# Layer 0's kept halves, a later flag branch and a shorter exact search in a two-layer attention and convolution kernel

## The chip, the cores and the metric

The kernel runs on one core of a Trainium2 chip. The metric is the time of one execution in microseconds (us) on the device. The engines are TensorE (PE, its weight loads PEld), VectorE (DVE), ScalarE (ACT), GpSimd (POOL) and SyncE (SP), which here issues the DMA transfers.

## The reference

2048 tokens of width 1024 pass two layers and a final norm. Layer 0 ("even") is sparse attention with 8 heads, in which an indexer selects the 256 best earlier positions for each token, beside a gated convolution of 31 taps; layer 1 ("odd") is a gated convolution of 3 taps. Cut to what matters here:

```python
def dsa_attention(q, k, v, q_idx, k_idx, w_idx):   # blocks of 128 queries
    dots = einsum('bqhd,bsd->bqhs', qib, kif)
    score = einsum('bqh,bqhs->bqs', wb, relu(dots))
    score = where(key_pos <= t, score, -inf)
    _, sel = lax.top_k(score, 256)
    ...                                  # softmax(q k) v over the selected positions

def odd_layer(h, w_in, conv_w, w_out):
    b_gate, c_gate, xin, gate = split(h @ w_in, 4)
    y = b_gate * causal_depthwise_conv(c_gate * xin, conv_w)
    return (y * silu(gate)) @ w_out

h = x
h = h + even_layer(rms_norm(h, g0), ...)
h = h + odd_layer(rms_norm(h, g1), ...)
return rms_norm(h, final_g)
```

## The kernel before, in words

Tokens are worked on in four chunks of 512 (16 blocks of 128). Weights and activations are fp32 values split into two fp16 halves, high and low, and each product of two of them takes three matmuls (`mm3`, L187 to L189, 24 matmuls for a projection onto 128 rows). Halves are named `xh`/`xl` (the normed input of layer 0), `mh`/`ml` (what goes into layer 0's output projection), `nh`/`nl` (the normed input of layer 1) and `yh`/`yl` (layer 1's product).

**Order.** The program is written as generators, each of which yields after a step. `weave(main, steps, (fill, rate), ...)` runs a main generator and, after each of its steps, so many steps of each fill as its rate says: `CN0` for the convolution of the next chunk, `R2` for the attention of chunk 1. `paced` ties an instruction to a matmul of the main generator, for the order alone. From this program a scheduler with a time model makes one list per engine, and an engine works off its list in order.

**Selection.** For most blocks the threshold of the 256 best is found by counting steps on ACT (L794) and a selection of candidates on DVE (L819 to L841), which ends by adding to `bad` whether a block was not settled. For blocks 2 and 3, and in a conditional fallback for all others, `general` (L276 to L317) finds it exactly: 31 bits of the threshold, one after the other; for each bit the scores of every block are compared with a trial threshold and counted (L292, once per block), the count is compared with 256 (L293), and the trial is kept or dropped (L304). Two more instructions per bit (L294, L295) keep the largest count below 256, and L302 turns the trial into a float's bits.

**From layer 0 to layer 1.** After layer 0's last attention, `fl`, `fps` and `fi` (L983 to L988) reduce `bad` to one flag. `last_gates` (L1117 to L1133) makes the last projections of layer 0 from chunk 3's halves, which it loads again from `xs_dr` into tiles of the pool `l1` (L1121, L1122). `out_even(0)` is the output projection of chunk 0, `norm_odd` the norm ahead of layer 1, whose `row_diag` ends in `rs_d` (L163) and whose `spread` multiplies that out (L169). Then the flag is loaded into a register on every engine (L1147) and a branch (L1148) skips the fallback, which isn't taken here; the keys and values of the attention are loaded (L1165, L1166). The loop over chunks follows: `odd` in 16 steps of two projections (48 matmuls) is woven with the attention of the next chunk (32 heads over four blocks; scores L1171, softmax L346 to L356 on DVE, ACT and POOL, transposing DMA L358, value products L379, transposed result L403). `out_even(1)` needs that attention's result as `mh`/`ml` (L182, L183).

Of the kernel before, what the change touches and what calls it, by code (L numbers as in the profile page):

```python
# [12 lines left out]
FP32 = mybir.dt.float32  # L13
# [8 lines left out]
P = 128  # L22
# [22 lines left out]
LOOK = 2  # L45
ATR = 3.5
CE, CX, CN0, CNR, R0, R1, R2 = 1.5, 3.0, 1.0, 0.85, 1.65, 1.65, 2.5
# [26 lines left out]
def trunk_kernel(ctx: ExitStack, tc: tile.TileContext, xT, pos, wE, woE, wO, woO, par, tab, outT):  # L74
# [38 lines left out]
    stg = ctx.enter_context(tc.tile_pool(name="stg", bufs=2))  # L113
    w_dr = {}
# [159 lines left out]
    def general(scs, get):  # L274
# [3 lines left out]
        def small(name, dt=FP32):  # L278
            return get(name, TT, dt)[:, 0:nb]

        cur, tr, bits, xm, acc = small("cur", I32), small("try", I32), small("bits", I32), small("xm", I32), small("acc", I32)
        cnt, cg, tmp, zero, izero = small("cnt"), small("cg"), small("tmp"), small("zero"), small("izero", I32)
        V.memset(cg, 0.0)
        V.memset(zero, 0.0)
        V.memset(izero, 0)
        V.memset(xm, 0x7FFFFFFF)
        V.memset(cur, -2 ** 31)

        def count(th):
            for n, b in enumerate(bl):  # L290
                junk = get("junk", wmax, BF16)
                V.tensor_scalar(out=junk[:, 0:(b + 1) * P], in0=scs[b], scalar1=th[:, n:n + 1], scalar2=0.0, op0=ALU.is_ge, op1=ALU.add, accum_out=cnt[:, n:n + 1])  # L292
            V.tensor_scalar(out=acc, in0=cnt, scalar1=float(TOPK), scalar2=None, op0=ALU.is_ge)  # L293
            V.scalar_tensor_tensor(out=tmp, in0=cnt, scalar=float(TOPK), in1=cnt, op0=ALU.is_lt, op1=ALU.mult)  # L294
            V.tensor_tensor(out=cg, in0=cg, in1=tmp, op=ALU.max)  # L295

        count(zero)
        V.copy_predicated(out=cur, mask=acc, data=izero)
        V.copy_predicated(out=xm, mask=acc, data=izero)
        for bit in range(30, -1, -1):  # L300
            V.tensor_scalar(out=tr, in0=cur, scalar1=1 << bit, scalar2=None, op0=ALU.bitwise_or)
            V.tensor_tensor(out=bits, in0=tr, in1=xm, op=ALU.bitwise_xor)  # L302
            count(bits.bitcast(FP32))
            V.copy_predicated(out=cur, mask=acc, data=tr)  # L304
        V.tensor_tensor(out=bits, in0=cur, in1=xm, op=ALU.bitwise_xor)
        thr = bits.bitcast(FP32)
# [121 lines left out]
    with ExitStack() as es:  # L428
        csp = es.enter_context(tc.tile_pool(name="csp", bufs=1))
        xp = es.enter_context(tc.tile_pool(name="xp", bufs=2))  # L430
# [549 lines left out]
        weave(rest(3, reload(3)), 99, (att, ATR))  # L980
        drain(att)

        fl = const.tile([P, 1], FP32, name="fl")  # L983
        V.tensor_reduce(out=fl, in_=bad, axis=mybir.AxisListType.X, op=ALU.max)
        fps = ps_m.tile([P, CH], FP32, name="ps_m")
        T.matmul(out=fps[:, 0:1], lhsT=ones, rhs=fl, start=True, stop=True)
        fi = const.tile([P, 1], I32, name="fi")
        V.tensor_scalar(out=fi, in0=fps[:, 0:1], scalar1=0.5, scalar2=None, op0=ALU.is_gt)  # L988
# [56 lines left out]

    def norm_all(x1, rb):
        nh = l1.tile([P, KD, CH], F16, name="nh", bufs=1)
        nl = l1.tile([P, KD, CH], F16, name="nl", bufs=1)
# [68 lines left out]
    def last_gates():  # L1117
        xh = l1.tile([P, KD, CH], F16, name="yh", bufs=1)
        xl = l1.tile([P, KD, CH], F16, name="yl", bufs=1)
        for k in range(0, KD, 4):  # L1120
            SP.dma_start(out=xh[:, k:k + 4, :], in_=xs_dr[NCH - 1][:, 0, k:k + 4])  # L1121
            SP.dma_start(out=xl[:, k:k + 4, :], in_=xs_dr[NCH - 1][:, 1, k:k + 4])  # L1122
# [21 lines left out]
    drain(late)  # L1144


    rv = nc.values_load(fi[0:1, 0:1], min_val=0, max_val=1)  # L1147
# [44 lines left out]
    for c in range(NCH):  # L1192
# [7 lines left out]
        yh = l1.tile([P, KD, CH], F16, name="yh", bufs=1)  # L1200
# [76 lines left out]
```

## Time and profile before

| | us |
|---|---|
| median of 3 runs | 2210.19 (2207.39 to 2213.84) |
| the profiled execution | 2207.73 |
| its span, first to last instruction | 2205.9 |
| PE busy in it | 1988.8 |
| DVE busy | 1657.8 |
| ACT busy | 1185.4 |
| POOL busy | 800.9 |

The profiled execution is one of its own; its time stands 1.8 us above its span and 2.5 us below the median of the runs. The mean granted clock of TensorE in it was 0.968 of full speed.

### The profile page before, as it was taken

The page shows a single profiled execution, that of the slowest core. Times are in us where ns is not written, and L with a number is a line of the kernel's source. Part 1 is how long each engine was busy: PE and PEld are TensorE (multiplying, and loading weights), DVE is VectorE, ACT ScalarE, POOL GpSimd, SP SyncE. Part 2 cuts the span into 40 slices and gives each one's busy share as a digit, 9 for nine tenths or more (in the row PEclk, how much of TensorE's full clock was granted, in tenths as well). Part 3 has the DMA queues.
Part 4 walks back from the last instruction along what each step waited for, and adds up shares of the span by engine and source line. Part 5 has one row for each costly group of instructions (what it writes and reads, how often), then busy time and mean ns, then how long its engine had stood idle before and what let it go on. Part 6 is the DMA issues. An engine that isn't in the chain of part 4 may idle for free. (4 is left out here: it accounts for less than half of the span.)

```text
span 2205.9 us, 34976 instructions
## 1 busy us (share of the span) xinstructions
PE 1988.8 (90%) x12252; PEld 1074.9 (49%) x12252; DVE 1657.8 (75%) x3580; ACT 1185.4 (54%) x2411; POOL 800.9 (36%) x761
## 2 busy tenths in 40 slices
PE   4877888898999898798998999999999999999997
PEld 3644464555454543344444444554554555444446
DVE  7999989999978694888874888874888887243224
ACT  5656665566577847467784654563554666121111
POOL 4765344435133321346662542441443455000000
PEclk9889999999999998999999999999999999999999
DMA  6445456333745376678896677776777788423234
GB/s 231 172 145 207 153 180 229 111 114 128 227 122 154 108 217 219 210 214 204 224 212 204 179 194 196 169 181 175 166 169 200 183 182 187 140 104 134 96 111 157
DMA packets 406052, 380.89 MB, mean 173 GB/s; under 512 B 313456, under 2 KB 333680, under 8 KB 385136
## 3 DMA queue, kind: packets, MB, share of 16 engines
q1 hardware_dynamic: 405872, 378.63, 60.5%
q8 instruction: 96, 1.57, 0.3%
q14 instruction: 84, 0.69, 0.1%
HBM read 216.45 MB, written 88.70 MB: 138 GB/s over the span
## 5 line engine op out<-in xcount | busy, mean ns | idle before, releaser
L356 POOL TENSOR_TENSOR pp<-lg,pp 128x512 f16<-128x512 f32 (+3 forms) x320 | 342.8, 1095 | 571.9 <-ACT pp L355 485.3
L187 PE MATMUL ps_w<-nh,wt 128*128 128x512 f16 x1024 | 391.1, 383 | 7.2 <-ACT wt L209 3.2
L188 PE MATMUL ps_w<-nl,wt 128*128 128x512 f16 x1024 | 392.0, 383 | 0.0
L189 PE MATMUL ps_w<-nh,wt 128*128 128x512 f16 x1024 | 389.2, 382 | 0.7 <-POOL wt L210 0.7
L187 PEld LDWEIGHTS <-wt 128*128 128x128 f16 x2112 | 208.3, 99 | 249.2 <-issue 23.4
L188 PEld LDWEIGHTS <-wt 128*128 128x128 f16 x2112 | 208.5, 99 | 242.1 <-issue 27.2
L189 PEld LDWEIGHTS <-wt 128*128 128x128 f16 x2112 | 208.6, 99 | 237.9 <-issue 11.2
L241 DVE SCALAR_TENSOR_TENSOR ps_c<-cin,cwt,ps_c 128x512 f32<-128x512 f32 x348 | 261.5, 752 | 30.8 <-ACT ps_c L239 26.9
L353 ACT ACTIVATE lg<-lg,m 128x512 f32<-128x512 f32 (+3 forms) x320 | 207.3, 649 | 120.4 <-DVE m L346 120.1
L210 POOL TENSOR_TENSOR wt<-w_stage,wt 128x512 f16<-128x512 f32 x136 | 167.9, 1241 | 262.3 <-ACT wt L209 248.5
L187 PE MATMUL ps_p<-xh,wt 128*128 128x512 f16 x480 | 185.1, 386 | 14.2 <-ACT th L222 5.9
L189 PE MATMUL ps_p<-xh,wt 128*128 128x512 f16 x480 | 184.0, 385 | 2.1 <-POOL wt L210 2.1
L188 PE MATMUL ps_p<-xl,wt 128*128 128x512 f16 x480 | 185.3, 386 | 0.0
L355 ACT CAST pp<-lg 128x512 f16<-128x512 f32 (+3 forms) x320 | 165.0, 550 | 21.9 <-DMA pt<-pp 17.2
L739 PE MATMUL ps_i<-ki,qst 128*128 128x512 f16 (+3 forms) x608 | 147.2, 363 | 32.7 <-ACT relu L741 32.1
L741 ACT ACTIVATE relu<-ps_i 128x1024 f32<-128x1024 f32 (+7 forms) x176 | 141.0, 811 | 65.0 <-DVE sc L743 39.3
L743 DVE SCALAR_TENSOR_TENSOR sc<-relu,wi,sc 128x1024 f32<-128x1024 f32 (+7 forms) x140 | 161.9, 1156 | 14.0 <-ACT relu L741 13.8
L187 PE MATMUL ps_p<-wt,xh 128*128 128x256 f16 (+1 forms) x608 | 167.9, 276 | 4.8 <-ACT u L598 2.5
L188 PE MATMUL ps_p<-wt,xh 128*128 128x256 f16 (+1 forms) x608 | 167.8, 276 | 0.6 <-POOL wt L210 0.6
L189 PE MATMUL ps_p<-wt,xl 128*128 128x256 f16 (+1 forms) x608 | 166.9, 276 | 0.1
L794 ACT ACTIVATE junk<-sc,t_x 128x640 bf16<-128x640 f32 (+5 forms) x84 | 118.8, 1414 | 65.2 <-DVE t_x L809 40.7
L1171 PE MATMUL ps_q<-kk,qs_a 128*128 128x512 f16 (+3 forms) x576 | 142.3, 356 | 4.4 <-DVE m L346 4.4
(293 smaller groups left out, 3851.2 us busy)
## 6 DMA issues: line engine op xcount, KB each, us to landing
wt<-w_in_wo_dram SPq DMA_DIRECT2D x48, 1024.0 KB, 5.1
wt<-w_in_we_dram SPq DMA_DIRECT2D x39, 1024.0 KB, 5.6
w_stage<-in_wo_dram SPq DMA_DIRECT2D x64, 256.0 KB, 3.5
w_in_wo_dram<-wt SPq DMA_DIRECT2D x16, 1024.0 KB, 4.9
wt<-w_in_woo_dram SPq DMA_DIRECT2D x16, 1024.0 KB, 5.0
w_in_we_dram<-wt SPq DMA_DIRECT2D x13, 1024.0 KB, 4.9
w_stage<-in_we_dram SPq DMA_DIRECT2D x48, 256.0 KB, 3.4
wt<-w_in_woe_dram SPq DMA_DIRECT2D x12, 1024.0 KB, 4.8
```

What stands on the lines that cost most here:

```text
L187: T.matmul(out=out, lhsT=sh(k), rhs=mh(k), start=k == 0, stop=False)
L188: T.matmul(out=out, lhsT=sh(k), rhs=ml(k), start=False, stop=False)
L189: state["mm"] = T.matmul(out=out, lhsT=sl(k), rhs=mh(k), start=False, stop=k == KD - 1)
L210: G.tensor_tensor(out=wt[:, 1, ks, :], in0=st, in1=wt[:, 0, ks, :], op=ALU.subtract)
L241: ins = V.scalar_tensor_tensor(out=out if t == CK - 1 else acc, in0=ci[:, t:t + CH], scalar=cwt[:, j, t:t + 1], in1=acc, op0=ALU.mult, op1 ...
L353: A.activation(out=e, in_=e, func=AF.Exp, bias=last, scale=-1.0, accum_out=blk["ss"][:, h, si:si + 1])
L355: A.copy(out=pp[:, 0:w], in_=e)
L356: eng.tensor_tensor(out=pp[:, w:2 * w], in0=e, in1=pp[:, 0:w], op=ALU.subtract)
L739: T.matmul(out=ps[:, r0:r0 + r], lhsT=qst[:, h, i * P:(i + 1) * P], rhs=ki[:, a, s0 + r0:s0 + r0 + r], start=a == 0, stop=a == 1)
L741: A.activation(out=rl[:, 0:w], in_=ps[:, 0:w], func=AF.Relu)
L743: V.scalar_tensor_tensor(out=sc[:, s0:s0 + w], in0=rl[:, 0:w], scalar=wi[:, b, h:h + 1], in1=tiny[:, s0:s0 + w] if h == 0 else sc[:, s0:s0 ...
L1171: ins = T.matmul(out=ps[:, 0:w], lhsT=qs[:, h, :], rhs=kk[:, a, s0:s0 + w], start=a == 0, stop=a == 1)
```

## The change

It does three things. (1) The pool `xp` of layer 0's halves lives on to the end of the kernel. The last pair that layer 0 loads (`held_last`) is handed to `last_gates`, which loads nothing any more, and the halves `nh`/`nl` and `yh`/`yl` of layer 1 are taken in turn from the same pool through `halves`. (2) The flag's reduction, its matmul and the branch stand after the first two steps of `odd` for chunk 0 (`ALONE`), so the loads of keys and values and the attention come behind that; those two steps are woven with the convolution only; the flag's matmul is tied to their last matmul. `R2` is 2.45 in place of 2.5. (3) `general` searches the float's own bits: it starts from -1, each trial flips one bit by exclusive or, and neither the mask `xm` nor the largest count below 256 is kept. The count above the threshold, which the last step needs, is taken once at the end, with `is_gt`.

```diff
@@ -43,8 +43,9 @@
 NCAND = 16
 NWT = 2
 LOOK = 2
+ALONE = 2
 ATR = 3.5
-CE, CX, CN0, CNR, R0, R1, R2 = 1.5, 3.0, 1.0, 0.85, 1.65, 1.65, 2.5
+CE, CX, CN0, CNR, R0, R1, R2 = 1.5, 3.0, 1.0, 0.85, 1.65, 1.65, 2.45
 ORDER = ('ggqgqg', 'ggqgqg', 'gggg', 'qq')
 EX = 1
 TQ, TP = 2, 4
@@ -111,6 +112,7 @@
     xs_dr = [dram.tile([P, 2, KD, CH], F16, name=f"xs_dr{c}") for c in range(NCH)]
     wp = ctx.enter_context(tc.tile_pool(name="wp", bufs=NWT))
     stg = ctx.enter_context(tc.tile_pool(name="stg", bufs=2))
+    xp = ctx.enter_context(tc.tile_pool(name="xp", bufs=2))
     w_dr = {}
     URGENT = {(wE.tensor.name, t) for t in (T_K, T_QI, T_KI)}
 
@@ -278,32 +280,29 @@
         def small(name, dt=FP32):
             return get(name, TT, dt)[:, 0:nb]
 
-        cur, tr, bits, xm, acc = small("cur", I32), small("try", I32), small("bits", I32), small("xm", I32), small("acc", I32)
-        cnt, cg, tmp, zero, izero = small("cnt"), small("cg"), small("tmp"), small("zero"), small("izero", I32)
-        V.memset(cg, 0.0)
+        cur, tr, acc = small("cur", I32), small("try", I32), small("acc", I32)
+        cnt, cg, zero, izero = small("cnt"), small("cg"), small("zero"), small("izero", I32)
         V.memset(zero, 0.0)
         V.memset(izero, 0)
-        V.memset(xm, 0x7FFFFFFF)
-        V.memset(cur, -2 ** 31)
-
-        def count(th):
+        V.memset(cur, -1)
+
+        def count(th, out, op):
             for n, b in enumerate(bl):
                 junk = get("junk", wmax, BF16)
-                V.tensor_scalar(out=junk[:, 0:(b + 1) * P], in0=scs[b], scalar1=th[:, n:n + 1], scalar2=0.0, op0=ALU.is_ge, op1=ALU.add, accum_out=cnt[:, n:n + 1])
+                V.tensor_scalar(out=junk[:, 0:(b + 1) * P], in0=scs[b], scalar1=th[:, n:n + 1], scalar2=0.0, op0=op, op1=ALU.add, accum_out=out[:, n:n + 1])
+
+        def keep(data):
             V.tensor_scalar(out=acc, in0=cnt, scalar1=float(TOPK), scalar2=None, op0=ALU.is_ge)
-            V.scalar_tensor_tensor(out=tmp, in0=cnt, scalar=float(TOPK), in1=cnt, op0=ALU.is_lt, op1=ALU.mult)
-            V.tensor_tensor(out=cg, in0=cg, in1=tmp, op=ALU.max)
-
-        count(zero)
-        V.copy_predicated(out=cur, mask=acc, data=izero)
-        V.copy_predicated(out=xm, mask=acc, data=izero)
+            V.copy_predicated(out=cur, mask=acc, data=data)
+
+        count(zero, cnt, ALU.is_ge)
+        keep(izero)
         for bit in range(30, -1, -1):
-            V.tensor_scalar(out=tr, in0=cur, scalar1=1 << bit, scalar2=None, op0=ALU.bitwise_or)
-            V.tensor_tensor(out=bits, in0=tr, in1=xm, op=ALU.bitwise_xor)
-            count(bits.bitcast(FP32))
-            V.copy_predicated(out=cur, mask=acc, data=tr)
-        V.tensor_tensor(out=bits, in0=cur, in1=xm, op=ALU.bitwise_xor)
-        thr = bits.bitcast(FP32)
+            V.tensor_scalar(out=tr, in0=cur, scalar1=1 << bit, scalar2=None, op0=ALU.bitwise_xor)
+            count(tr.bitcast(FP32), cnt, ALU.is_ge)
+            keep(tr)
+        thr = cur.bitcast(FP32)
+        count(thr, cg, ALU.is_gt)
         V.tensor_scalar(out=cg, in0=cg, scalar1=-1.0, scalar2=float(TOPK), op0=ALU.mult, op1=ALU.add)
         for n, b in enumerate(bl):
             W = (b + 1) * P
@@ -427,7 +426,6 @@
 
     with ExitStack() as es:
         csp = es.enter_context(tc.tile_pool(name="csp", bufs=1))
-        xp = es.enter_context(tc.tile_pool(name="xp", bufs=2))
         e1 = es.enter_context(tc.tile_pool(name="e1", bufs=2))
         p0 = es.enter_context(tc.tile_pool(name="p0", bufs=2))
         cvp = es.enter_context(tc.tile_pool(name="cvp", bufs=1))
@@ -977,15 +975,9 @@
         r2 = rest(2, reload(2))
         weave(r2, 99, (cn0, CE), (att, ATR))
         drain(cn0)
-        weave(rest(3, reload(3)), 99, (att, ATR))
+        held_last = reload(3)
+        weave(rest(3, held_last), 99, (att, ATR))
         drain(att)
-
-        fl = const.tile([P, 1], FP32, name="fl")
-        V.tensor_reduce(out=fl, in_=bad, axis=mybir.AxisListType.X, op=ALU.max)
-        fps = ps_m.tile([P, CH], FP32, name="ps_m")
-        T.matmul(out=fps[:, 0:1], lhsT=ones, rhs=fl, start=True, stop=True)
-        fi = const.tile([P, 1], I32, name="fi")
-        V.tensor_scalar(out=fi, in0=fps[:, 0:1], scalar1=0.5, scalar2=None, op0=ALU.is_gt)
 
 
     mx = ctx.enter_context(tc.tile_pool(name="mx", bufs=1, reuse_waits="tile"))
@@ -1043,9 +1035,11 @@
             state["gate"] = None
             return norm_all(x1, rb)
 
+    def halves():
+        return xp.tile([P, KD, CH], F16, name="xh"), xp.tile([P, KD, CH], F16, name="xl")
+
     def norm_all(x1, rb):
-        nh = l1.tile([P, KD, CH], F16, name="nh", bufs=1)
-        nl = l1.tile([P, KD, CH], F16, name="nl", bufs=1)
+        nh, nl = halves()
         for k in range(KD):
             xn = l1.tile([P, CH], FP32, name="xi")
             V.scalar_tensor_tensor(out=xn, in0=x1[:, k, :], scalar=g1[:, k:k + 1], in1=rb, op0=ALU.mult, op1=ALU.mult)
@@ -1115,11 +1109,7 @@
         return l1.tile([P, KD, CH], FP32, name="x1"), l1.tile([P, CH], FP32, name="ssum", bufs=1)
 
     def last_gates():
-        xh = l1.tile([P, KD, CH], F16, name="yh", bufs=1)
-        xl = l1.tile([P, KD, CH], F16, name="yl", bufs=1)
-        for k in range(0, KD, 4):
-            SP.dma_start(out=xh[:, k:k + 4, :], in_=xs_dr[NCH - 1][:, 0, k:k + 4])
-            SP.dma_start(out=xl[:, k:k + 4, :], in_=xs_dr[NCH - 1][:, 1, k:k + 4])
+        xh, xl = held_last
 
         def chan(wt, z):
             ps = ps_w.tile([P, CH], FP32, name="ps_w")
@@ -1142,8 +1132,19 @@
     drain(even)
     n = norm_odd(x1, acc, late)
     drain(late)
-
-
+    yh, yl = halves()
+    main = odd(*n, yh, yl)
+    weave(main, ALONE, (cnv, CN0))
+
+
+    fl = const.tile([P, 1], FP32, name="fl")
+    V.tensor_reduce(out=fl, in_=bad, axis=mybir.AxisListType.X, op=ALU.max)
+    fps = ps_n.tile([P, CH], FP32, name="ps_m")
+    state["gate"] = state["mm"]
+    paced(T.matmul(out=fps[:, 0:1], lhsT=ones, rhs=fl, start=True, stop=True))
+    state["gate"] = None
+    fi = const.tile([P, 1], I32, name="fi")
+    V.tensor_scalar(out=fi, in0=fps[:, 0:1], scalar1=0.5, scalar2=None, op0=ALU.is_gt)
     rv = nc.values_load(fi[0:1, 0:1], min_val=0, max_val=1)
     with tc.If(rv > 0):
         with tc.tile_pool(name="fb", bufs=1) as fb:
@@ -1197,9 +1198,9 @@
             weave(out_even(c, *m[c], x1, acc), 99, (cnv, CNR), (att, R0))
             n = norm_odd(x1, acc, late, (cnv, CNR), (att, R1))
             weave(late, 99, (cnv, CNR), (att, R1))
-        yh = l1.tile([P, KD, CH], F16, name="yh", bufs=1)
-        yl = l1.tile([P, KD, CH], F16, name="yl", bufs=1)
-        weave(odd(*n, yh, yl), 99, (cnv, CNR if c else CN0), (att, R1 if c else R2))
+            yh, yl = halves()
+            main = odd(*n, yh, yl)
+        weave(main, 99, (cnv, CNR if c else CN0), (att, R1 if c else R2))
         late = out_odd(c, x1, yh, yl, 2 if c + 1 == NCH else 1)
         drain(att)
         drain(cnv)
```

DVE near layer 1's first norm, before, in the program's order. `rs_a`, `rs_r` and `rs_t` are steps of the norm's reciprocal root, `fi` is the flag. The names behind the operation are output and inputs, then the output's shape.

```order
L148 SCALAR_TENSOR_TENSOR rs_t<-rs_t,rs_a 128x4
L149 SCALAR_TENSOR_TENSOR rs_r<-rs_t,rs_r 128x4
L147 TENSOR_TENSOR rs_t<-rs_r 128x4
L148 SCALAR_TENSOR_TENSOR rs_t<-rs_t,rs_a 128x4
L149 SCALAR_TENSOR_TENSOR rs_r<-rs_t,rs_r 128x4
L147 TENSOR_TENSOR rs_t<-rs_r 128x4
L988 TENSOR_SCALAR fi<-ps_m 128x1
L148 SCALAR_TENSOR_TENSOR rs_t<-rs_t,rs_a 128x4
L1147 TENSOR_LOAD fi
L1148 COMPARE_AND_BRANCH
```

And after the change, the same norm up to its end, where `fl` is the flag's reduction and `xi` the first normed rows of layer 1:

```order
L1141 TENSOR_REDUCE fl<-bad 128x1
L149 TENSOR_TENSOR rs_t<-rs_r 128x4
L150 SCALAR_TENSOR_TENSOR rs_t<-rs_t,rs_a 128x4
L151 SCALAR_TENSOR_TENSOR rs_r<-rs_t,rs_r 128x4
L149 TENSOR_TENSOR rs_t<-rs_r 128x4
L150 SCALAR_TENSOR_TENSOR rs_t<-rs_t,rs_a 128x4
L151 SCALAR_TENSOR_TENSOR rs_r<-rs_t,rs_r 128x4
L149 TENSOR_TENSOR rs_t<-rs_r 128x4
L150 SCALAR_TENSOR_TENSOR rs_t<-rs_t,rs_a 128x4
L151 SCALAR_TENSOR_TENSOR rs_r<-rs_t,rs_r 128x4
L165 SCALAR_TENSOR_TENSOR rs_d<-id_62,rs_r 128x512
L1045 SCALAR_TENSOR_TENSOR xi<-x_9786,par_sb,ps_m 128x512 x2
```

The flag's conversion, its load and the branch are gone from the middle of the norm; the line numbers after the change are one to two higher in the helpers (L163 is L165).

PE around the flag, before: the last products of `last_gates`, the flag's matmul, the branch, the norm's product and the first products of layer 1:

```order
L188 LDWEIGHTS wt
L188 MATMUL ps_w<-yl,wt 128x512
L189 LDWEIGHTS wt
L189 MATMUL ps_w<-yh,wt 128x512
L986 MATMUL ps_m<-fl,ones 128x1
L1147 TENSOR_LOAD fi
L1148 COMPARE_AND_BRANCH
L1148 UNCONDITIONAL_BRANCH x2
L169 MATMUL ps_m<-rs_d,ones 128x512
L187 LDWEIGHTS wt
L187 MATMUL ps_w<-nh,wt 128x512
```

And around the branch after the change, where the tiles of layer 1's first halves are now called `xh` and `xl`:

```order
L190 LDWEIGHTS wt
L190 MATMUL ps_w<-xl,wt 128x512
L191 LDWEIGHTS wt
L191 MATMUL ps_w<-xh,wt 128x512
L1148 TENSOR_LOAD fi
L1149 COMPARE_AND_BRANCH
L1149 UNCONDITIONAL_BRANCH x2
L189 LDWEIGHTS wt
L189 MATMUL ps_w<-xh,wt 128x512
L190 LDWEIGHTS wt
```

The branch stands among the products of layer 1's third step (117 of them are ahead of it, and 149 ahead of the first score product), the norm's product is far above it, and the flag's matmul 21 products above it.

PE near the end of `odd` for chunk 0, before: `a_nat` is the attention's last result, transposed here, and 68 products of `odd` still follow:

```order
L187 LDWEIGHTS wt
L187 MATMUL ps_w<-nh,wt 128x512
L188 LDWEIGHTS wt
L188 MATMUL ps_w<-nl,wt 128x512
L403 MATMUL ps_m<-id_62,a_nat 128x128 x4
L189 LDWEIGHTS wt
L189 MATMUL ps_w<-nh,wt 128x512
L187 LDWEIGHTS wt
L187 MATMUL ps_w<-nh,wt 128x512
L188 LDWEIGHTS wt
L188 MATMUL ps_w<-nl,wt 128x512
```

And after the change:

```order
L378 MATMUL ps_v<-vv,pt 128x128
L378 LDWEIGHTS pt
L378 MATMUL ps_v<-vv,pt 128x64
L378 LDWEIGHTS pt
L378 MATMUL ps_v<-vv,pt 128x128
L402 MATMUL ps_m<-id_62,a_nat 128x128 x4
L189 LDWEIGHTS wt
L189 MATMUL ps_w<-mh,wt 128x512
L189 LDWEIGHTS wt
L189 MATMUL ps_w<-mh,wt 128x512
```

The transposed result now stands at the very end, behind the last product of `odd`, the last score products and 48 value products (`ps_v`), and `out_even(1)` (`mh`, `ml`) follows it directly.

## Rows read from the trace of the kernel before

**Rows 1.** page, part 1: engine, busy us, share of the span, instructions.

```profile
PE 1988.8 (90%) x12252; PEld 1074.9 (49%) x12252; DVE 1657.8 (75%) x3580; ACT 1185.4 (54%) x2411; POOL 800.9 (36%) x761
```

**Rows 2.** windows: stretch, length; busy us of each engine (x count); clock, DMA share.

```profile
117.00:300.00 183.00, 144.14 (x808) 78.45 (x807) 180.25 (x554) 115.06 (x207) 85.66 (x81) 0.90 0.52 183
...
870.00:930.00 60.00, 56.25 (x263) 25.40 (x261) 55.98 (x96) 26.07 (x44) 19.78 (x16) 1.00 0.57 194
...
940.00:950.00 10.00, 8.51 (x27) 3.01 (x26) 8.80 (x14) 5.12 (x9) 0.17 (x1) 0.64 0.74 279
```

**Rows 3.** PE's waits, 117 to 300 us: sum in us, times, longest.

```profile
PE ps_t L633 <- DVE stk L620: 11.9, 3, 5.6
...
PE ps_i L739 <- ACT relu L741: 10.8, 10, 3.2
```

**Rows 4.** page, part 5: busy, mean ns | idle before it, main releaser.

```profile
L741 ACT ACTIVATE relu<-ps_i 128x1024 f32<-128x1024 f32 (+7 forms) x176 | 141.0, 811 | 65.0 <-DVE sc L743 39.3
```

**Rows 5.** PE's waits, 848 to 960 us.

```profile
PE ps_m L169 <- DVE rs_d L163: 10.2, 1, 10.2
...
PE ps_w L187 <- DMA yh<-xs_dr: 9.5, 1, 9.5
```

**Rows 6.** DVE's groups by form, 117 to 283 us: busy us, mean ns.

```profile
L295 DVE TENSOR_TENSOR s_cg<-s_cg,s_tmp 128x2 f32<-128x2 f32 x32 | 8.9, 278 | 0.0
...
L294 DVE SCALAR_TENSOR_TENSOR s_tmp<-s_cnt 128x2 f32<-128x2 f32 x32 | 8.0, 249 | 0.0
...
L302 DVE TENSOR_TENSOR s_bits<-s_try,s_xm 128x2 int32<-128x2 int32 x31 | 7.8, 250 | 0.5
```

**Rows 7.** DVE's timeline in the search: start, us, instruction.

```profile
260.16 0.17 DVE L293 TENSOR_SCALAR s_acc<-s_cnt 128x2 int32<-128x2 f32 x1
...
260.76 0.16 DVE L302 TENSOR_TENSOR s_bits<-s_try,s_xm 128x2 int32<-128x2 int32 x1
...
260.96 0.61 DVE L292 TENSOR_SCALAR_CACHE_REDUCE mk<-cv,s_bits 128x384 bf16<-128x384 f32 x1
```

**Rows 8.** timelines, ACT, then DVE, near the norm; in brackets the idle time before.

```profile
863.35 0.63 ACT L208 ACTIVATE w_stage<-w_stage 128x512 f32<-128x512 f32 x1 [3.04 <-DMA w_stage<-in_woe_dram]
...
864.54 1.89 ACT L794 ACTIVATE junk<-sc,t_x 128x1920 bf16<-128x1920 f32 x1
...
934.65 0.63 ACT L208 ACTIVATE w_stage<-w_stage 128x512 f32<-128x512 f32 x1 [6.39 <-SPq L1148]
...
936.83 0.35 DVE L149 SCALAR_TENSOR_TENSOR rs_r<-rs_t,rs_r 128x4 f32<-128x4 f32 x1 [5.14 <-DVEq L1148]
...
937.21 1.67 DVE L163 SCALAR_TENSOR_TENSOR rs_d<-id,rs_r 128x512 f32<-128x512 f32 x1
```

**Rows 9.** timelines of PE, DVE and ACT, chunk 1's attention.

```profile
942.57 1.01 PE L187 MATMUL ps_w<-nh,wt 128*128 128x512 f16 x2 [1.49 <-ACT nh L182]
...
955.17 0.92 PE L1171 MATMUL ps_q<-kk,qs_a 128*128 128x512 f16 x5
...
1147.45 0.59 PE L1171 MATMUL ps_q<-kk,qs_a 128*128 128x512 f16 x2
...
1151.87 0.74 DVE L346 CUSTOM_DVE_ANT_0 lg<-ps_q,mb_a,m 128x512 f32<-128x512 f32 x1
...
1153.74 0.71 ACT L353 ACTIVATE lg<-lg,m 128x512 f32<-128x512 f32 x1
...
1157.52 0.60 ACT L355 CAST pp<-lg 128x512 f16<-128x512 f32 x1
...
1172.97 0.69 DVE L183 TENSOR_TENSOR ml<-a_nat,mh 128x512 f16<-128x512 f32 x1 [0.69 <-ACT mh L182]
...
1189.51 0.38 PE L187 MATMUL ps_w<-mh,wt 128*128 128x512 f16 x1
...
1199.65 0.38 PE L189 MATMUL ps_w<-mh,wt 128*128 128x512 f16 x1
```

**Rows 10.** line L1147, the flag's load: duration in ns, start us.

```profile
L1147 ACTq TENSOR_LOAD <-fi x1: 1422/1422/1422, 931.6 to 931.6; - x1
```

## The prediction

> **What bounds the kernel now.** I read the engine totals first, then windows by stage, then who PE waits for, then timelines around the two places that the diff edits. PE is busy 1988.8 of 2205.9 us, DVE 1657.8 [rows 1]: over the whole PE is the bound, so only PE's idle time can be won. Windows show two stages in which DVE is the bound instead: from 117 to 300 us DVE is busy 180.25 of 183 and PE 144.14; from 870 to 930 us DVE has 55.98 of 60 [rows 2]. The first holds the exact search that `general` runs for blocks 2 and 3; the second ends in layer 0's last selection and the norm ahead of the odd layer. PE's two long waits in the first stage sum to 22.7 us: one goes to DVE directly [rows 3], the one for relu at second hand, since ACT's relu mostly waits for DVE's L743 [rows 4]. Around the second place PE has two waits, 9.5 us for the reloaded halves and 10.2 us for the norm's `rs_d` [rows 5].
>
> **Search, 31 bits.** L294, L295 and L302 go, 8.0 + 8.9 + 7.8 = 24.7 us of profile time in 95 instructions [rows 6]. That overstates them, since a DVE instruction's time overlaps its neighbour's. In an undisturbed bit six small operations lie between the start of L293 at 260.16 and the next count at 260.96, 0.80 us; one that needs its predecessor's result costs 0.20, by the starts of L302 and of that count [rows 7]. Three such steps remain (L293, the copy, L301): 0.60. So 0.20 × 31 = 6.2 us are sure. Further, 24.7 − 95 × 0.16 = 9.5 us of rows 6 are excess over the 0.16 of an undisturbed one: waits put on tiny operations. They go with the instructions (9.5) or the next instruction takes them over (0); no row decides, so I take half, 4.8. Against it stand two new counts at the end: the 384 wide one took 0.61 [rows 7], the 512 wide one by proportion 0.8, together 1.4, less two initial operations of 0.16 that go: −1.1. DVE saves 6.2 + 4.8 − 1.1 = 9.9, bounds 5.1 and 14.6. PE was idle 38.9 us in that stage [rows 2]; since DVE is busy 98% of it but only 22.7 of the 38.9 are traced to it by rows, I pass on the middle between 22.7 / 38.9 = 0.58 and 0.98: 0.78 × 9.9, **−7.7 us, bounds −3 (0.58 × 5.1) and −14.6**.
>
> [...]
>
> **Reload.** The loads of layer 0's last halves (2 MB) and PE's 9.5 us behind them [rows 5] vanish. But DVE is late next: it is 93% busy from 870 to 930 [rows 2], and `rs_d` stands behind the selection tail in its order, before and after (first pair of fences). What can move `rs_d`: first, the selection waits for ACT's counts, the last two of which stand behind an L208 that waited 3.04 us for its load [rows 8]; ACT's order lets them pass it now, so they come 0 to 4.2 us sooner (3.04 and the 1.19 from the start of L208 to that of the count after it), and I take 3.0, the wait alone. Second, DVE's idle time there, 60 − 55.98 = 4.0 at most, of which I take 3.5, since most of it is waits on PE's and the queue's results that come earlier. Third, the branch stood inside the norm's chain: DVE idles 5.14 for it [rows 8]; it is behind the norm now. `rs_d` ended at 937.21 + 1.67 = 938.88; it will end 3.0 + 3.5 + 5.1 = **11.6 earlier (5.1 to 13.3)**, at 927.3. With the 3.7 us from there to the first odd matmul at 942.57 [rows 9] kept, the odd layer begins at 931.0.
>
> **Branch, in its new place.** It stands after 117 odd matmuls (second pair of fences), no longer in a pause, so PE pays. The load of the flag started at 931.6 and took 1.42 on ACT [rows 10]; ACT worked again 3.05 after that start, DVE 5.2 [rows 8]. PE had nothing to do then, so its own restart isn't seen. Bounds are 1.5, the load alone, and 5.2; I take ACT's 3.05. A stall can cost clock too: after the pause of before the granted clock was 0.64 from 940 to 950 [rows 2], that is 7.2 us at the lower of its two levels, 2.6 of them ahead of the first matmul; half of the other 4.6, 2.3, is lost. After so much shorter a stall I add 0.9 (0 to 2.3): **+4, 1.5 to 7.5**. The flag's own chain (`bad`, which stands ahead of `rs_d` on DVE, and one matmul) is covered by 96 odd matmuls.
>
> [...]
>
> **Attention of chunk 1.** Its score products can't be issued until the branch is past: 149 odd matmuls stand ahead of them, before only 48. One matmul takes (1199.65 − 1189.51) / 47 = 0.2157 us, first and last start of 48 in a row [rows 9]: 149 × 0.2157 = 32.1, with 2.3 for the low clock at the beginning and 4 for the branch 38.4. Scores begin at 931.0 + 38.4 = 969.4, before at 955.17. From the first to the last score group it took 1147.45 − 955.17 = 192.3 with 592 odd matmuls in between by the order; after, 619 and 5.8 us more: 1167.5. What follows the last score was covered before, by 128 odd matmuls until `out_even(1)` began at 1189.51. After, there are only 48 value products and four transposes (third pair of fences), and then `out_even(1)` wants the result. From the last score group's start to the end of `ml` were 1172.97 + 0.69 − 1147.45 = 26.2 us. Two waits in it are behind other work, most of which will be over: L346 starts 3.8 after the score group's end (1151.87 − 1148.04), and between its exponential and its first cast ACT does 3.1 of other things (1154.45 to 1157.52, [rows 9]). 26.2 − 6.9 = 19.3; lower end 16.1 (from that cast on), upper end 26.2. With 2.3 of low clock behind this pause `out_even(1)` begins as if at 1167.5 + 19.3 + 2.3 = 1189.1: **−0.4, ±8**. So of 11.6 us won at the norm nearly all is paid again here. From `out_even(1)` on, PE's order is the same row for row. Orders that changed elsewhere, and the rate of 2.45, I set at nothing, ±4 by choice: PE has work in those stretches, and its order there moves by rows of the same kind.
>
> **Sum.** −7.7 − 0.4 = −8.1 on the profiled execution's 2207.7 is 2199.6. That execution stands 2.5 below the median of the runs shown, so the forecast is 2202.1, given as **2202**.
>
> **Rivals.** (A) *Full price*: both parts give their better ends, the search 14.6 and the boundary 0.4 + 1.7 (`rs_d` 13.3 early) + 2.5 (branch at 1.5) + 3.2 (a tail of 16.1) + 2.3 (no clock lost) = 10.1: 2210.2 − 24.7 = 2185.5. For it speak PE's real stalls [rows 5], against it DVE's load between them. (B) *The stalls only change place*: the wait for the reload becomes one for DVE, the small operations lie beside waits on GpSimd, and 3 us of the search and 2 of the boundary remain: 2205.2. For it: DVE at 93 and 98%, where freeing PE alone does nothing. (C) *Slower*: the attention of chunk 1 falls behind the last odd step. Three heads' value products stand behind the last odd matmul, and a head takes 192.3 / 32 = 6.0 us; if these heads have still to be worked off after the last score, the tail is 19.3 + 18 = 37.3, and the boundary comes out at −0.4 + 18 = +17.6: 2210.2 − 7.7 + 17.6 = 2220.1. It decides, that is, gives the time of before, from a tail of 19.3 + 8.1 = 27.4 us. For it: all of that attention starts 14 us later. Against: with odd steps gone, ACT, POOL and DVE are free there.
>
> **How the numbers follow.** Chances: forecast 0.50 (own range 2191 to 2208), A 0.15, B 0.20, C 0.15. A measurement of this kernel can tell about 0.3% (6.6 us) from no change, so faster means below 2203.6 and slower above 2216.8. Faster: 0.38 of the forecast's 0.50, whose time lies near that line, all of A, 0.05 of B: 0.58. Slower: 0.12 of C, 0.01 of the forecast: 0.13. Same: the rest, 0.29. The range reaches from just under A's time to 2214, where a tail between the forecast's and C's ends.
>
> **What would show it.** Right: a search that ends 7 to 12 us earlier, with fewer small operations of unchanged length; no wait of PE for a load of halves; `rs_d` some 12 us earlier; PE idle about 3 us at the branch and 15 to 25 us ahead of `out_even(1)`. Wrong: a search that ends as late as before, a tail of over 27 us ahead of `out_even(1)`, or a new wait of over 4 us behind it.

## The result and the profile after

The change made the kernel slower. Its median is 2226.53 us (4 runs, 2223.46 to 2227.91) against 2208.82 for the kernel before (4 runs, 2207.39 to 2213.84), a ratio of 1.007 with a 95% interval of 1.0049 to 1.009. The forecast was 2202, with a range to 2214.

The profiled execution took 2226.34 us. The page's engine totals show what kind of loss it is:

```profile
PE 1988.8 (89%) x12252; PEld 1071.2 (48%) x12252; DVE 1659.4 (75%) x3485; ACT 1177.1 (53%) x2407; POOL 803.5 (36%) x761
```

PE does the same work in the same time as before [rows 1]; the span grew by 18.7 us of idle time. Windows of the changed kernel (stretch and length, then busy time of PE, PEld, DVE, ACT and POOL, then clock) show where not to look, the search, and where to look, the attention of chunk 1 from its first score product to `out_even(1)`:

```profile
117.00:300.00 183.00, 148.59 (x877) 84.54 (x876) 173.60 (x474) 116.76 (x209) 85.80 (x81) 0.93 0.55 192
...
957.70:1209.20 251.50, 197.99 (x1191) 95.52 (x1192) 166.09 (x317) 160.06 (x366) 130.25 (x120) 0.92 0.72 192
```

In the first, PE is 4.5 us busier than before and DVE less loaded [rows 2]. In the second, PE is idle for 53.5 us. The timelines of DVE and PE give the milestones (start, length, instruction, and in brackets the idle time ahead of it); the matmuls named `xh` are those that were `nh`:

```profile
914.76 0.69 DVE L165 SCALAR_TENSOR_TENSOR rs_d<-id,rs_r 128x512 f32<-128x512 f32 x1
...
920.92 1.01 PE L189 MATMUL ps_w<-xh,wt 128*128 128x512 f16 x2 [3.29 <-ACT xh L184]
...
957.72 1.15 PE L1172 MATMUL ps_q<-kk,qs_a 128*128 128x512 f16 x6
...
1192.54 1.03 PE L1172 MATMUL ps_q<-kk,qs_a 128*128 128x512 f16 x4
...
1203.01 0.82 PE L378 MATMUL ps_v<-vv,pt 128*128 128x128 f16 x8 [8.09 <-DMA pt<-pp]
...
1209.23 1.01 PE L189 MATMUL ps_w<-mh,wt 128*128 128x512 f16 x2 [1.43 <-ACT mh L184]
```

Against [rows 8, 9]: `rs_d` ends at 915.45, 23.4 us earlier than before, and the odd layer starts 21.6 earlier. The first score starts 2.6 later than before (957.7 against 955.2), the last one 45.1 later, and `out_even(1)` 19.7 later. What follows `out_even(1)` takes 1015.4 us to the end of the span, before 1016.4. So all of the gain and 20 us more are lost on the way from the first odd matmul to `out_even(1)`. The windows from the first to the last score, before and then after the change, say where:

```profile
955.17:1147.45 192.28, 179.16 (x1095) 89.40 (x1094) 151.61 (x306) 144.75 (x335) 120.19 (x112) 0.96 0.86 211
957.72:1192.54 234.82, 192.84 (x1136) 91.68 (x1137) 160.52 (x304) 154.89 (x355) 127.99 (x118) 0.93 0.73 192
```

Between the scores PE is idle for 42.0 us, before 13.1. Behind the last score, up to `out_even(1)`, it is idle for 11.6, before 7.5. PE's waits between 920.92 and 1209.23 name what it waited for (sum, times, longest):

```profile
PE ps_v L378 <- DMA pt<-pp: 21.3, 10, 8.1
PE ps_w L189 <- ACT wt L211: 18.8, 10, 4.9
PE ps_w L191 <- POOL wt L212: 4.6, 9, 1.1
PE ps_m L171 <- DVE rs_d L165: 3.8, 1, 3.8
```

The same view of the kernel before, between 942.57 and 1189.51:

```profile
PE ps_v L379 <- DMA pt<-pp: 12.3, 13, 2.1
PE ps_w L187 <- ACT wt L209: 3.2, 2, 2.2
...
PE ps_w L189 <- POOL wt L210: 0.7, 3, 0.3
```

PE waits 19.5 us more for weights (both halves of `wt`) and 9 more for transposes, of which one wait of 8.1 stands behind the last score, ahead of the last heads' value products. Between the scores alone the changed kernel waits 23.4 us for weights and 12.8 for transposes. Before, the view from 955.17 to 1147.45 names no wait for weights at all:

```profile
PE ps_v L379 <- DMA pt<-pp: 11.4, 11, 2.1
PE ps_m L403 <- DVE a_nat L399: 1.3, 1, 1.3
```

So most of what PE loses between the scores is waits for weights.

### The profile page after: what moved, and what is told of

Same layout as the page of the kernel before. It is cut to its first block, busy times and chain, and to the rows that moved or that the text cites. A ratio compares the mean times of both kernels' runs of the same rounds, so it can differ in the third digit from the quotient of the medians.

```text
span 2224.6 us, 34871 instructions
## 1 busy us (share of the span) xinstructions
PE 1988.8 (89%) x12252; PEld 1071.2 (48%) x12252; DVE 1659.4 (75%) x3485; ACT 1177.1 (53%) x2407; POOL 803.5 (36%) x761
## 5 line engine op out<-in xcount | busy, mean ns | idle before, releaser
L189 PE MATMUL ps_w<-xh,wt 128*128 128x512 f16 (+1 forms) x1376 | 514.3, 375 | 26.3 <-ACT wt L211 18.8
L190 PE MATMUL ps_w<-xl,wt 128*128 128x512 f16 (+1 forms) x1376 | 514.6, 374 | 0.2 <-DVE xl L185 0.2
L191 PE MATMUL ps_w<-xh,wt 128*128 128x512 f16 (+1 forms) x1376 | 508.9, 374 | 4.6 <-POOL wt L212 4.6
L189 PEld LDWEIGHTS <-wt 128*128 128x128 f16 x2112 | 209.5, 99 | 257.0 <-ACT wt L211 25.5
L741 DVE SCALAR_TENSOR_TENSOR sc<-relu,wi,sc 128x1024 f32<-128x1024 f32 (+7 forms) x140 | 164.5, 1175 | 14.2 <-ACT relu L739 14.1
L354 ACT CAST pp<-lg 128x512 f16<-128x512 f32 (+3 forms) x320 | 163.9, 547 | 18.4 <-DMA pt<-pp 16.4
L189 PE MATMUL ps_p<-wt,xh 128*128 128x256 f16 (+1 forms) x608 | 164.3, 270 | 5.2 <-ACT u L596 2.3
L190 PE MATMUL ps_p<-wt,xh 128*128 128x256 f16 (+1 forms) x608 | 164.3, 270 | 0.0
L378 PE MATMUL ps_v<-vv,pt 128*128 128x64 f16 (+1 forms) x2016 | 116.9, 209 | 37.2 <-DMA pt<-pp 37.0
```

The source lines that it names most:

```text
L189: T.matmul(out=out, lhsT=sh(k), rhs=mh(k), start=k == 0, stop=False)
L190: T.matmul(out=out, lhsT=sh(k), rhs=ml(k), start=False, stop=False)
L191: state["mm"] = T.matmul(out=out, lhsT=sl(k), rhs=mh(k), start=False, stop=k == KD - 1)
L354: A.copy(out=pp[:, 0:w], in_=e)
L741: V.scalar_tensor_tensor(out=sc[:, s0:s0 + w], in0=rl[:, 0:w], scalar=wi[:, b, h:h + 1], in1=tiny[:, s0:s0 + w] if h == 0 else sc[:, s0:s0 ...
```

## The experiments

The ratios of the experiments are against runs of the kernel before on the same chip, where its median was 2214.4, 2212.1 and 2211.1 us in the three groups of four kernels. The **stretch** is the time from the first odd matmul of chunk 0 to the first matmul of `out_even(1)` in the profiled execution; "order" counts odd matmuls ahead of the first score, between first and last score, and behind the last; "weights" is the sum of PE's waits for `wt` between first and last score, in us.

| kernel | median us | ratio (95%) | first odd | stretch | order | weights |
|---|---|---|---|---|---|---|
| before | | 1 | 942.6 | 246.9 | 48 / 592 / 128 | 0 |
| changed | 2226.5 | 1.007 (1.0049 to 1.009) | 920.9 | 288.3 | 149 / 619 / 0 | 23.4 |
| p1_search | 2197.3 | 0.993 (0.9907 to 0.9952) | 919.8 | 258.6 | 48 / 588 / 132 | 8.0 |
| p2_held | 2214.9 | 1.0004 (0.9989 to 1.002) | 936.6 | 259.0 | 48 / 576 / 144 | 9.4 |
| p3_branch | 2246.2 | 1.0163 (1.0128 to 1.0198) | 932.5 | 291.5 | 149 / 619 / 0 | 25.6 |
| p4_search_held | 2190.8 | 0.9902 (0.9874 to 0.993) | 924.2 | 247.7 | 48 / 592 / 128 | 0 |
| p5_alone0 | 2207.8 | 0.9983 (0.9971 to 0.9994) | 921.7 | 268.6 | 88 / 545 / 135 | 17.1 |
| p6_alone1 | 2209.7 | 0.9989 (0.9974 to 1.0004) | 922.7 | 264.8 | 101 / 619 / 48 | 12.0 |
| p8_rate32 | 2208.7 | 0.9989 (0.9973 to 1.0005) | 920.3 | 272.9 | 149 / 451 / 168 | 16.8 |
| p9_delay | 2217.9 | 1.0029 (1.0015 to 1.0043) | 924.1 | 272.7 | 144 / 624 / 0 | 16.6 |
| p10_delay_rate32 | 2199.8 | 0.9947 (0.993 to 0.9964) | 923.2 | 257.0 | 144 / 456 / 168 | 2.5 |
| p11_no_branch | 2214.2 | 1.0016 (1.0004 to 1.0028) | 919.8 | 275.5 | 144 / 624 / 0 | 21.8 |
| p13_kv_first | 2217.3 | 1.0033 (1.0021 to 1.0045) | 921.6 | 275.8 | 144 / 624 / 0 | 15.2 |
| p16_rate32_early | 2194.2 | 0.9923 (0.9898 to 0.9947) | 923.6 | 252.5 | 48 / 465 / 255 | 0 |

The kernels with a stretch of 247 to 259 us wait at most 9.4 us for weights between the scores, those with 265 to 276 us 12.0 to 21.8, and the two with 288 and more over 23. These are single profiles, and that the two go together shows no cause by itself.

### Which part loses

The first four kernels take the change apart: the new `general` alone; `xp`, `halves` and `held_last` alone; the later flag and branch with `ALONE` and the rate alone; and the first two together.

The third is, in short, this edit of the kernel before:

```diff
-CE, CX, CN0, CNR, R0, R1, R2 = 1.5, 3.0, 1.0, 0.85, 1.65, 1.65, 2.5
+CE, CX, CN0, CNR, R0, R1, R2 = 1.5, 3.0, 1.0, 0.85, 1.65, 1.65, 2.45
...
+    main = odd(*n, yh, yl)
+    weave(main, ALONE, (cnv, CN0))
+    fl = const.tile([P, 1], FP32, name="fl")
...
+    fps = ps_n.tile([P, CH], FP32, name="ps_m")
...
     rv = nc.values_load(fi[0:1, 0:1], min_val=0, max_val=1)
```

> The kernel before with the shorter search alone. Two theories of the 17.7 us that the change lost. Late attention: the 41 us by which the stretch from the first odd matmul to out_even(1) grew (246.9 to 288) come from the attention of chunk 1 starting two odd steps later. Late weights: they come from the odd layer starting some 21 us earlier, before its weights are converted, so that PE waits for wt. Both expect the search to end about 15 us earlier here (267 in place of 282 us). Late attention: 2190 to 2200, as the stretch of chunk 1 keeps its 247 us within 5. Late weights: about 2200, a part of the gain is given back in waits for wt in chunk 1.

> The kernel before with the halves kept and shared alone, flag and branch in their old place. Late attention: the 9.5 us wait for the reload goes, part of it comes back on DVE, chunk 1's stretch stays at 247 within 5; 2200 to 2206. Late weights: the odd layer starts 5 to 10 us earlier and waits for wt by as much; 2208 to 2218.

> The kernel before with the flag, the branch and the attention's start two odd steps later and the rate 2.45, nothing else. Late attention: chunk 1's stretch grows to 275 to 290 us, PE's order has no odd matmul behind the last score; 2230 to 2245. Late weights: the layer starts hardly earlier, so the weights are as they were: 2205 to 2214.

> The changed kernel with flag, branch and rate as before, so search and kept halves without the delay. Late attention: both gains and no loss, 2183 to 2195. Late weights: the odd layer starts about as early as in the changed kernel and waits for wt by 15 us or more; 2205 to 2220.

The search alone gains 0.7% and the late branch alone loses 1.6%, with the stretch at 291.5, about as in the changed kernel, though its odd layer starts 12 us later there. (Its time and its stretch lie just above what late attention gave, 2245 and 290.) Search and halves without the late branch gain 1%, and the odd layer that starts 18 us earlier than before keeps its stretch of 247.7. So the loss isn't the effect of an early start on the weights, and the late attention stands. Two expectations of it missed. The halves alone gain nothing (1.0004) and fall where late weights had put them (2208 to 2218). And the stretch was to keep its length within 5 us, but grew by 12 in p2_held and by 12 in p1_search too, though that kernel's time came out as expected. In the stretch of p2_held PE waits 11.1 us for ACT's `wt`, in that of p1_search 9.4; with search and halves together it waits 1.8:

```profile
PE ps_v L377 <- DMA pt<-pp: 15.1, 12, 3.5
PE ps_w L190 <- POOL wt L211: 2.0, 3, 1.6
PE ps_m L170 <- DVE rs_d L164: 1.8, 1, 1.8
PE ps_w L188 <- ACT wt L210: 1.8, 2, 1.5
```

These are PE's waits in the stretch of p4_search_held. Why either part alone comes out otherwise stays open.

### Delay, branch or rate

The late branch does three things at once: it delays the attention by two odd steps, it stands in the midst of the odd layer, and it comes with a rate that ends the attention behind the last odd matmul.

The edits, in the order of the expectations below; the first three are made on the changed kernel (the first with `R2` at 2.5), the fourth on p4_search_held with `R2` at 2.45:

```diff
-    weave(main, ALONE, (cnv, CN0))
```

```diff
-ALONE = 2
+ALONE = 1
```

```diff
-CE, CX, CN0, CNR, R0, R1, R2 = 1.5, 3.0, 1.0, 0.85, 1.65, 1.65, 2.45
+CE, CX, CN0, CNR, R0, R1, R2 = 1.5, 3.0, 1.0, 0.85, 1.65, 1.65, 3.2
```

```diff
+        main = odd(*n, yh, yl)
+        if c == 0:
+            weave(main, 2, (cnv, CN0))
...
```

> The changed kernel with flag and branch behind the norm but ahead of the odd layer's first step, rate 2.5; the order has 88 odd matmuls ahead of the first score and 135 behind the last. Three theories of the 32 to 36 us that the moved branch costs. Delay: the attention has two steps fewer to spread over, and each step with it gets longer. Branch: the branch in the midst of the odd layer disturbs what the engines had prepared. Rate: 2.45 a step ends the attention behind the last odd matmul, and nothing covers its chain. Delay and rate: 2188 to 2198, near the kernel with search and halves alone. Branch: 2195 to 2205, as it costs its own 4 us and some.

> The changed kernel with one odd step ahead of the branch in place of two; the order has 101 odd matmuls ahead of the first score and 48 behind the last. Delay: about half of the loss, 2203 to 2212. Branch: as slow as the changed kernel, 2220 to 2230. Rate: 2195 to 2205, since 48 matmuls are a cover of 10 us for a tail of 17.

> The changed kernel with the attention's rate at 3.2 a step in place of 2.45; the order has 451 odd matmuls between first and last score and 168 behind the last. Rate: 2190 to 2202. Delay: the steps with attention get longer still and give back what the cover brings, 2212 to 2228. Branch: 2215 to 2228.

> Search and kept halves with flag and branch in their old place, but the first two odd steps woven without attention and the rate 2.45, as in the changed kernel; the order has 144 odd matmuls ahead of the first score and none behind the last. Delay and rate: as slow as the changed kernel less the branch's own few us, 2215 to 2226. Branch: 2188 to 2198.

p9_delay has the changed kernel's order around the attention but not its branch there, and loses most of what the changed kernel loses (ratio 1.0029 against 0.9902 without the delay). So the branch isn't the main cause. But p5_alone0, without any delay by steps, is 0.8% slower than p4_search_held, more than any theory allowed: its flag's matmul shares a PSUM tile with the norm, and its branch stands 12 us into the odd layer (933.3 against 921.7). Its first score also stands behind 88 odd matmuls in place of 48, so this kernel doesn't tell the branch's place from a delay. p6_alone1 (2209.7) fell where delay had put it, with half of the loss; branch and rate were off by 10 and by 5 us. For p8_rate32 none of the three was right alone; the rate wins back half.

### Each one apart

p10_delay_rate32 is p9_delay, and p16_rate32_early is p4_search_held, each with `R2` at 3.2. p11_no_branch and p13_kv_first are these edits of the changed kernel:

```diff
-    rv = nc.values_load(fi[0:1, 0:1], min_val=0, max_val=1)
-    with tc.If(rv > 0):
...
```

```diff
+    kk = kvp.tile([P, 2, S], F16, name="kk")
+    vv = kvp.tile([P, NB, 2, HD], F16, name="vv")
+    SP.dma_start(out=kk, in_=k_dr)
+    SP.dma_start(out=vv, in_=v_dr)
     yh, yl = halves()
     main = odd(*n, yh, yl)
     weave(main, ALONE, (cnv, CN0))
...
```

> Search and kept halves, flag and branch in their old place, the first two odd steps without attention, but 3.2 in place of 2.45 attention steps to each odd step: the order has 144 odd matmuls ahead of the first score, 456 in between and 168 behind the last. If the delay costs because nothing covers the end of the attention's chain, the cover brings it back: 2193 to 2203. If it costs because each odd step with attention gets longer, the denser steps lose what the cover brings: 2212 to 2222.

> The changed kernel without the branch and the fallback behind it; the flag is still computed, but not read. If the branch in the midst of the odd layer costs only its own stall, 2220 to 2224. If it costs a late restart of the weights' chain too (loads, casts on ACT, low halves on POOL) that the odd steps never make up for, 2206 to 2216.

> The changed kernel with the keys' and values' loads (1.5 MB) ahead of the two odd steps and so ahead of the branch; in the fallback, which is not executed, two scratch tiles share a place to make room. If the loads that the branch releases at once, all on SP's queue, keep the next weights' loads waiting, the weights come back sooner behind the branch: 2212 to 2221. If not, 2223 to 2229.

> Search and kept halves with flag and branch in their old place and no delay, but the rate 3.2: 48 odd matmuls ahead of the first score, 465 in between, 255 behind the last. If an attention that ends early is as good as one that ends with some cover, 2187 to 2197, as with 2.5. If denser steps cost by themselves, 2200 to 2210.

All four fell where one of the theories had put them. **Cover:** with the same delay, 168 odd matmuls behind the last score instead of none bring 0.8% (1.0029 to 0.9947, 18 us). PE's waits in the stretch of p9_delay, and then of p10_delay_rate32:

```profile
PE ps_v L377 <- DMA pt<-pp: 19.3, 10, 8.5
PE ps_w L188 <- ACT wt L210: 11.9, 7, 3.3
PE ps_w L190 <- POOL wt L211: 4.7, 6, 1.3
PE ps_m L401 <- DVE a_nat L397: 3.2, 2, 1.6
```

```profile
PE ps_v L377 <- DMA pt<-pp: 15.9, 13, 2.5
PE ps_w L188 <- ACT wt L210: 9.7, 6, 3.8
PE ps_w L188 <- ACT xh L183: 1.5, 1, 1.5
PE ps_w L188 <- ACT cs L1066: 1.5, 2, 1.2
PE ps_w L190 <- POOL wt L211: 1.3, 4, 0.5
```

The one wait of 8.5 us for the last heads' transposes is gone, the transposed results' too, and the waits for weights are 5.6 shorter. So cover isn't the whole of it: PE's idle time in the stretch falls from 43.2 to 29.5 us, and some 40% of that are weights that come sooner, for a reason that isn't shown. The delay that remains costs 0.45%, 10 us (0.9902 to 0.9947), together with the denser rate. p16_rate32_early and p10_delay_rate32, which differ in the delay alone, lie 0.24%, 5 us, apart, and their intervals overlap. The rate as such is no gain: 3.2 without the delay is 0.9923, not better than 0.9902 with 2.5, where 128 matmuls are cover enough.

**Branch:** without it the changed kernel is 0.54%, 12 us, faster (1.007 to 1.0016). At the rate 3.2 its place costs 0.42%, 9 us (p8_rate32 against p10_delay_rate32). With only the keys' and values' loads taken out from behind it, 0.37%, 8 us. What the branch holds back is seen on SP's queue of the changed kernel, and then on ACT:

```profile
950.21 0.33 SPq L1166 DMA_DIRECT2D kk<-k_dr  x1
950.69 0.33 SPq L1167 DMA_DIRECT2D vv<-v_dr  x1
951.06 0.43 SPq L327 DMA_DIRECT2D qs_a<-q_dr  x1
951.93 0.32 SPq L333 DMA_DIRECT2D mb_a<-mb_dr  x1
952.36 0.37 SPq L205 DMA_DIRECT2D w_stage<-in_wo_dram  x1
```

```profile
948.45 0.63 ACT L210 ACTIVATE w_stage<-w_stage 128x512 f32<-128x512 f32 x1 [2.49 <-SPq L1149]
...
958.84 0.63 ACT L210 ACTIVATE w_stage<-w_stage 128x512 f32<-128x512 f32 x1 [5.27 <-DMA w_stage<-in_wo_dram]
```

SP issues nothing from the branch until 950.21, then four loads for the attention, and the next piece of a weight only at 952.36. ACT gets a piece 10.4 us after the one ahead of it, while a step wants four pieces. In the kernel before, the same loads went out from 937.73 on, while PE stood waiting for the norm anyway.

How much of the 12 us goes this way isn't shown. In p13_kv_first PE's waits for weights between the scores are 8.2 us shorter (15.2 against 23.4), as the queue would have it. But in p11_no_branch, without any branch, they are hardly shorter (21.8). There the waits for transposes between the scores fell, from 12.8 to 5.5.

## Why the prediction was wrong

**The step that failed** is in the part on chunk 1's attention: "From the first to the last score group it took 1147.45 − 955.17 = 192.3 with 592 odd matmuls in between by the order; after, 619 and 5.8 us more". I took the pace of before as a price per odd matmul and added 27 of them. Measured were 234.8, 36.7 more than the 198.1 forecast. Of these, 28.9 are PE's idle time between the scores (42.0 against 13.1); the rest is busy time, at a granted clock of 0.93 in place of 0.96 and with 14 further matmuls that aren't odd ones. Nearly all of the added idle time is waits for weights, 23.4 us where there had been none, and no term of the sum held them. Two odd steps ahead of the attention bring most of them with the branch in its old place (p9_delay, 16.6), and they stay when the branch is taken out (p11_no_branch, 21.8). At the rate 3.2 there are 2.5 with the branch in its old place (p10_delay_rate32) and 16.8 with the late one (p8_rate32). So delay, rate and branch all bear on them; why the weights come late stays open. The rate of 2.45, which I set at nothing, belongs to the same step: at 3.2 the changed kernel is 18 us faster (p8_rate32).

The changed kernel lies 37 us above p4_search_held: 10 for delay and denser rate (p10_delay_rate32), 18 for a rate that leaves no odd matmul behind the last score (p9_delay), 9 for the branch in the midst of the odd layer. Each of the three is uncertain by 5 to 7 us. They are steps from kernel to kernel, in whole times, and not the parts of the 36.7, though the sums are nearly the same.

**Around it**, the same part was near. First odd matmul to first score: 38.4 forecast, 36.8 measured. The tail from the last score to `out_even(1)`: 19.3 forecast, 2.3 of low clock behind it not counted, and 16.7 measured. The two levels of the granted clock that the prediction counts with are in the windows: before, 0.50 from 931 to 947 us and 1.00 from 948 to 952; after, 0.50 from 1200 to 1212 and 1.00 from 1214 to 1218. So the exposed tail was seen and priced; the time between the scores wasn't. The signs of being wrong named the search and the tail, and not that time.

**Search.** Mis-sized. DVE was to save 9.9 us, 5.1 to 14.6. The last bit's copy, before and then after, starts 15.1 us earlier (the last two figures are first and last start):

```profile
L304 DVE COPY_PREDICATED s_cur<-s_acc,s_try x31: 149/158/1105, 122.6 to 282.0; 128x2 int32<-128x2 int32 x31
L296 DVE COPY_PREDICATED s_cur<-s_acc,s_try x31: 147/164/1090, 121.6 to 266.9; 128x2 int32<-128x2 int32 x31
```

The two new counts stand behind that copy. The first instruction on the scores behind them (L311, before L312) starts at 268.61 in place of 282.77, so 14.2 are saved with the counts in. PE was to get 0.78 of the saving, 7.7; the kernel with the search alone gains 0.7%, 15 us, by its interval 11 to 21, so about as much as DVE. (The upper bound of 14.6 for PE is DVE's whole saving; with the prediction's own 0.98 it would be 14.3.) Of the 9.5 us of excess in [rows 6] half was to pass on to other instructions. The groups by form from 110 to 283 us, before and then after (busy us, mean ns), show how much did:

```profile
L293 DVE TENSOR_SCALAR s_acc<-s_cnt 128x2 int32<-128x2 f32 x32 | 10.3, 321 | 0.3
L301 DVE TENSOR_SCALAR s_try<-s_cur 128x2 int32<-128x2 int32 x31 | 8.7, 282 | 0.0
L304 DVE COPY_PREDICATED s_cur<-s_acc,s_try 128x2 int32<-128x2 int32 x31 | 10.2, 328 | 0.0
...
L295 DVE TENSOR_SCALAR s_acc<-s_cnt 128x2 int32<-128x2 f32 x32 | 13.4, 419 | 0.2
L301 DVE TENSOR_SCALAR s_try<-s_cur 128x2 int32<-128x2 int32 x31 | 10.3, 333 | 0.6
L296 DVE COPY_PREDICATED s_cur<-s_acc,s_try 128x2 int32<-128x2 int32 x31 | 9.1, 294 | 0.5
```

The three grew by 3.1 and 1.6 and shrank by 1.1: 3.6 passed on, 5.9 went. With that the sum is 6.2 + 5.9 − 1.1 = 11.0; the other 3 us I can't place. The long ones among the tiny operations end with POOL's instructions. Before, from 117 to 283 us, 35 of the search's 189 small operations (L293 to L295, L301, L302 and L304) took over 0.3 us, and each of the 35 ended within 0.05 us of the end of a POOL instruction; of the 154 shorter ones one did:

```profile
142.07 1.16 POOL L210 TENSOR_TENSOR wt<-w_stage,wt 128x512 f16<-128x512 f32 x1 [2.27 <-ACT wt L209]
142.18 1.07 DVE L302 TENSOR_TENSOR s_bits<-s_try,s_xm 128x2 int32<-128x2 int32 x1
...
148.21 1.65 POOL L210 TENSOR_TENSOR wt<-w_stage,wt 128x512 f16<-128x512 f32 x1 [4.98 <-ACT wt L209]
148.76 1.13 DVE L301 TENSOR_SCALAR s_try<-s_cur 128x2 int32<-128x2 int32 x1
```

After, from 117 to 269 us, 26 of 95 took over 0.3 us, all with such an end, and none of the other 69 has one. L293 and L301 (after: L295 and L301), which read one tensor, are among the long ones in both kernels: 13 of the 35, 19 of the 26. That they waited is the prediction's reading; why they end so isn't shown.

**Reload.** The order of the milestones held: PE's stall went, DVE was late next, `rs_d` came early. It ended 23.4 us earlier, at 915.45. The reload and the branch's move were to bring 11.6 of that (5.1 to 13.3). But with the search alone it ends 21.8 earlier, at 917.06, though PE still waits 9.8 us for the reloaded halves there:

```profile
916.37 0.69 DVE L163 SCALAR_TENSOR_TENSOR rs_d<-id,rs_r 128x512 f32<-128x512 f32 x1
```

With the halves alone it ends 5.9 earlier (932.96), with search and halves 18.4 (920.52). So beside the search this term was worth 1.6 us in these profiles and not 11.6. Whether the halves are worth anything at the end stays between nothing (alone) and 6 us (0.993 to 0.9902 beside the search, with intervals that overlap).

**Branch.** PE was to lose 4 us. It lost 1.08, in one wait for DVE; DVE stood 4.03 and ACT 2.49. The compare-and-branch instruction itself took 45 to 228 ns on the five engines, before and after. Of the 3.05 us that the prediction took from ACT, 1.42 are the flag's load [rows 10]; the other 1.63 are not the branch instruction's own (50 ns on ACT): the view puts ACT's idle time there to SP. What the branch's place costs in whole times, 9 to 12 us (p9_delay, p11_no_branch), was in no term beyond these 4.

**Rivals.** C, slower, had the sign and a time (2220.1) near the measured one, but not the place: it wanted a tail of 37 us behind the last score, and the tail is 16.7. Its time came near by luck. Of A's parts the search did come near its 14.6 (15 us in p1_search), the boundary did not. Of B's mechanism, the long small operations do end with POOL's instructions, but with those 15 us the search brought far more than 3. The chance of 0.13 for slower was too small, because an attention that runs beside other work was priced as if its pace were given.

The lowest ratio of these kernels is that of p4_search_held, search and halves with flag and branch where they were: 0.9902 of the kernel before (0.9874 to 0.993), 0.9833 of the changed one by the two ratios. The intervals of p16_rate32_early and p1_search overlap with it.

## What to carry to other kernels

The attention that ran beside PE's own work had no fixed price per matmul. Before moving the start of such a chain, ask what will still be there to cover its end: here 128 matmuls behind the last score hid a tail of 17 us and more, and two steps of delay used them up. Ask too what else will be short of time once the order is denser: here most of the loss was waits for weights, which nobody had priced. A branch that an engine hardly notices (1.08 us on PE) can still cost more (9 to 12 us): look at what the loads behind it will be asked for at once, and whether the loads ahead of it have run far enough in advance.

## What the runs showed of the hardware

PE passed the branch without a pause of its own. In the changed kernel its sequencer loaded the flag at 945.8 and branched at 947.2:

```profile
L1148 PEldq TENSOR_LOAD <-fi x1: 1377/1377/1377, 945.8 to 945.8; - x1
L1149 PEldq COMPARE_BRANCH  x1: 228/228/228, 947.2 to 947.2; - x1
```

Matmuls ran on all the while. By the count from 920.92, the last of the 117 ahead of the branch started at 949.11, so it had been handed on before. Three that stand behind the branch followed without a gap, and the first gap is a wait for DVE:

```profile
949.11 0.38 PE L191 MATMUL ps_w<-xh,wt 128*128 128x512 f16 x1
...
949.75 0.38 PE L191 MATMUL ps_w<-xh,wt 128*128 128x512 f16 x1
951.22 0.38 PE L189 MATMUL ps_w<-xh,wt 128*128 128x512 f16 x1 [1.08 <-DVE th L1077]
```

So some 3.7 us of matmuls covered a load of 1.38 us and the branch. DVE and ACT stood 4.03 and 2.49 there; what they waited for beyond the load isn't shown.
